# Hybrid encoder layer on one core: query and key/value latents computed together, block by block of the input features

## The chip, the cores and the metric

One core of one Trainium2 chip runs the whole layer. The metric is the device time of one execution in microseconds, the median of several timed runs. A profile comes from one execution of its own, recorded by the hardware profiler; its span is somewhat shorter than the timed figure, because the timed figure takes in what lies around the span.

## The reference

One layer of an encoder, for 512 tokens of 1024 features, everything float32:

```python
h = RMSNorm(x); z = h @ W_in     # columns: q-latent 256 | kv-latent 256 | rotary key 64 |
                                 #          HGRN2 q 512 | f_fwd 512 | f_bwd 512 | i 512 | gate 512
q = rms_norm(rms_norm(c_q, g_qa) @ w_qb, g_qn)       # 4 heads of 128 + 64 rotary
k, v from rms_norm(c_kv, g_kva) @ w_kvb              # 4 heads of 128 (+ shared rotary key), v 128
A = softmax(q k^T * 192**-0.5) v                     # dense, both directions in time
B = HGRN2: gated linear recurrence, chunks of 64, one scan forward and one backward, summed
x += concat(A, B) @ W_o
x += SwiGLU(RMSNorm(x))                              # inner width 2816
x += sigmoid(RMSNorm(x) @ W_pg) * (p[layer] @ W_pp)
```

The gates of HGRN2 are f = lower + (1 - lower) * sigmoid(z), where `lower` comes from a softmax over two rows of learned bounds.

## The kernel before

**Precision.** Every float32 factor is split into a high and a low part (`split`: ScalarE copies or scales to the high part, VectorE subtracts to get the low part). A product of two such factors is three products on TensorE (`mm3`, L137 to L139: hi·hi, hi·lo, lo·hi). A chunk of weights is loaded by the SyncE queue (SP) into one of four `raw` buffers and split into one of three pairs of buffers `whi`, `wlo` (`weights`).

**Order.** Each engine runs its instructions in one fixed order. This order is found before the launch by a scheduler that goes by the program's dependences and by its own picture of durations, so an edit in one place can move instructions elsewhere. An engine stands still while its next instruction waits, and all that is queued behind it stands too.

**Front part.** x lies transposed in eight blocks of 128 features by 512 tokens (`xT[k]`, 256 KB each). VectorE, ScalarE and GpSimd (POOL) set constants, and TensorE does `WARM` products of constants (`warm`). Then:

1. the query's latents `cq` in two banks, as features by tokens: per block k the parts `hh`, `hl` of x times gain (`vec` holds the gains), and 2 x 3 products of 512 columns. w_q comes in five loads, for blocks (0), (1), (2,3), (4,5), (6,7);
2. constants `cst`, `row`, `pos` are loaded, and POOL makes the sum of the squares of x (`sq`, `sqacc`);
3. the key/value latents `ckv` in four banks, as tokens by features: per block 4 x 3 products of 320 columns, with w_kv in three loads;
4. `token_rstd` turns the squares into 1/rms (`ss`), the latents are normed (`squares`, `cT`, `ctok`), POOL and ScalarE make the rotary tables, and the bounds of the gates (`lower`) are worked out from columns 30 to 45 of `vec`.

**Middle part** (some 40 to 300 us). Two streams share TensorE: the attention (`rk`, `ropeT`, `qkT` are transposes; `ks`, `kl`, `qs` are the rotary parts of key and query, `qkh`, `qkl` the other parts; `s` are scores, `p` their exponentials, `pT` these transposed, `av` the values) and the projections of HGRN2 (`wi`, one tile of 128 columns is 24 products against a weight chunk of 1024 columns). VectorE serves both: it subtracts the low parts of the weights (`wlo`, L131), evacuates tiles (`z`), runs the scans of the gates (L636, L638), copies their decays in small pieces (`dm`, `dt`), finishes `qs` (L484), and takes maxima of scores.

**Last part.** Output projection, feed-forward (`ff`, `dn`), per-layer gate (`pg`).

Of the kernel before, what the change touches and what calls it, by code (L numbers as in the profile page):

```python
# [18 lines left out]
KT = 8  # L19
# [5 lines left out]
# shares of the two streams  # L25
# [5 lines left out]
WARM = 7  # L31
# [5 lines left out]
# columns of the packed per-partition vectors  # L37
V_MIX, V_FFN, V_PLE, V_QA, V_KVA, V_QN, V_KN, V_LB, V_HGO = 0, 8, 16, 24, 26, 28, 29, 30, 46
NV = 50
# columns of the packed rows (the same for every partition)  # L40
R_QN, R_KN = 0, 64
NR = 128
# columns of the constants that depend on shapes alone
# [11 lines left out]
class Slots:  # L55
    """Tiles of one size, handed out by hand: the one that has been free longest comes next."""
# [19 lines left out]
    def part(self, prefix, n):  # L76
        """Slots of their own from the free ones."""
        s = Slots(self.pool, 0, self.prefix)
        s.free.extend(self.free.popleft() for _ in range(n))
        s.count = 1000 * ord(prefix)  # L80
        return s
# [7 lines left out]
def merge(streams):  # L89
    """Runs generators side by side, by the shares of their totals that they have yielded. One that  # L90
    yields a condition waits until it holds."""
# [16 lines left out]
def v3(t, a, b=None):  # L108
    """A tile's 512 columns as (a, b)."""
    return t.rearrange("p (a b) -> p a b", a=a)  # L110
# [3 lines left out]
def layer_kernel(ctx: ExitStack, tc: tile.TileContext, io, out):  # L114
# [11 lines left out]
    # ---------------------------------------------------------------- helpers  # L126
    def split(hi, lo, src, scale=None, eng=dve):
        """src (times a scale per partition) = hi + lo, each exact in float32r."""
# [14 lines left out]
    def weights(src, cols, lo_eng=None):  # L143
        """A chunk of weights [128, cols]: its parts hi and lo."""
# [14 lines left out]
    def rsqrt_mean(o, ss, n):  # L159
        """o = (ss / n + eps) ** -0.5, for a few columns."""  # L160
# [5 lines left out]
    def token_rstd(sq, keep=None):  # L166
        """From sums of squares [128 of the features, tokens]: 1/rms by token, tokens on
        partitions [128, 4] and on columns, the same on every partition [128, 512]."""
# [6 lines left out]
        # the diagonal matrices of 1 / rms, summed over the partitions  # L175
# [13 lines left out]
    def squares(acc, src, first):  # L189
        """acc += src ** 2"""  # L190
# [8 lines left out]
    # ---------------------------------------------------------------- inputs  # L199
# [3 lines left out]
    sp.dma_start(vec, io["vec"])  # L203
# [7 lines left out]
    # loads the activation engine's table while the first inputs are under way  # L211
    act.activation(small.tile([P, 1], F32, tag="first", name="first"), mhalf[:, :1], AF.Exp)

    # ---------------------------------------------------------------- input projection, latents
    # the query's latents, features on partitions
    hT = [(A.get(f"hh{k}", F32R), A.get(f"hl{k}", F32R)) for k in range(KT)]
    cq = [B.get(f"cq{m}") for m in range(2)]
    # the tensor engine's clock rises while it is busy
# [4 lines left out]
    for ks in ((0,), (1,), (2, 3), (4, 5), (6, 7)):  # L223
        w = weights(io["w_q"][:, ks[0] * 256 : (ks[-1] + 1) * 256], len(ks) * 256)
        for k in ks:
            if k:
                sp.dma_start(xT[k], io["xT"][k])
            split(hT[k][0], hT[k][1], xT[k], vec[:, V_MIX + k : V_MIX + k + 1])
            for m in range(2):
                o = (k - ks[0]) * 256 + m * P  # L230
                mm3(cq[m], cut(w, o, o + P), hT[k], k == 0, k == KT - 1)
# [10 lines left out]
    for k in range(KT):  # L242
        t = A.get("sq") if k else sq
        pool.tensor_tensor(t, xT[k], xT[k], ALU.mult)
        if k:
            pool.tensor_tensor(sq, sq, t, ALU.add)
            A.put(t)
    A.put(*xT)

    # those of key and value and the rotary key, tokens on partitions  # L250
    ckv = [B.get(f"ckv{j}") for j in range(NT)]
    for c, ks in enumerate(((0, 1, 2), (3, 4, 5), (6, 7))):
        w = weights(io["w_kv"][:, ks[0] * 320 : (ks[-1] + 1) * 320], len(ks) * 320)
        for k in ks:
            for j in range(NT):
                o = (k - ks[0]) * 320
                mm3(ckv[j][:, :320], cut(hT[k], j * P, (j + 1) * P), cut(w, o, o + 320), k == 0, k == KT - 1)
# [16 lines left out]
    # ---------------------------------------------------------------- rotary tables  # L274
# [17 lines left out]
    # cos(r) = sin(pi / 2 - |r|)  # L292
# [9 lines left out]
    def rope(eng, o, x, c, s, t1, t2):  # L302
        """o = x * [cos, cos] + [x2, x1] * [-sin, sin], all [128, a, 64]"""
# [5 lines left out]
    # ---------------------------------------------------------------- lower bounds of the gates  # L309
    lb = vec[:, V_LB : V_LB + 16]  # L310
# [13 lines left out]
    # ================================================================ latent attention  # L324
# [4 lines left out]
    def attention():  # L329
        """Emits the attention in pieces; yields the tensor engine's time for each."""  # L330
        # 1 / rms of the latents, with the one of the input
        sc = cpool.tile([P, 2 * NT], F32, name="sc")  # by token: query, key and value
# [28 lines left out]
        # the shared rotary key, with its gains, turned  # L361
# [8 lines left out]
        def wsmall(name, cols):  # L370
            """A small matrix of two chunks, two halves each."""
# [11 lines left out]
        # keys and values; per head, tokens on partitions: [128, tile, 128]  # L383
# [3 lines left out]
        rt = [A.get(f"rk{j}") for j in range(NT)]  # rotary parts by tile: [128, (key, query) x head, 64]  # L387
# [164 lines left out]
    q, kk, bb = {}, {}, {}  # L552
    gg, vv = [], []

    # chunks of weights for the dense stream, one ahead of its use
    wlist = deque()
    ahead = deque()
    nd = [0]
# [520 lines left out]
```

## Time and profile before

| what | us |
|---|---|
| timed runs | 723.92 median (723.46, 723.92, 724.87) |
| span of the profiled execution | 721.8 |
| TensorE busy | 703.6 (97%) |
| VectorE busy | 439.3 (61%) |
| ScalarE busy | 309.2 (43%) |
| GpSimd busy | 135.8 (19%) |

The profile gives the profiled execution's time as its span, 721.8 us; no other time of that execution is shown. The median of the timed runs lies 2.1 us above it. Busy shares are means over the span, so they say little about a stage. "Idle before, releaser" is the time an engine stood and what ended it. PEclk is TensorE's granted clock as a share of full speed.

### The profile page before, as it was taken

The page shows a single profiled execution, that of the slowest core. Times are in us where ns is not written, and L with a number is a line of the kernel's source. Part 1 is how long each engine was busy: PE and PEld are TensorE (multiplying, and loading weights), DVE is VectorE, ACT ScalarE, POOL GpSimd, SP SyncE. Part 2 cuts the span into 40 slices and gives each one's busy share as a digit, 9 for nine tenths or more (in the row PEclk, how much of TensorE's full clock was granted, in tenths as well). Part 3 has the DMA queues.
Part 4 walks back from the last instruction along what each step waited for, and adds up shares of the span by engine and source line. Part 5 has one row for each costly group of instructions (what it writes and reads, how often), then busy time and mean ns, then how long its engine had stood idle before and what let it go on. Part 6 is the DMA issues. An engine that isn't in the chain of part 4 may idle for free.

```text
span 721.8 us, 9167 instructions
## 1 busy us (share of the span) xinstructions
PE 703.6 (97%) x3516; PEld 588.5 (82%) x3516; DVE 439.3 (61%) x733; ACT 309.2 (43%) x573; POOL 135.8 (19%) x126
## 2 busy tenths in 40 slices
PE   8999997998999999999999999999999999999997
PEld 6888885897878888788888888888888888888886
DVE  8954469988999984386545334435433444456573
ACT  5566785576554635355233222223222223244341
POOL 7983577010543511001000000000000000000000
PEclk9999999999999999999999999999999999999999
DMA  8432112111034221033232322232233232233211
GB/s 282 167 114 93 59 36 81 59 30 60 15 103 156 60 78 59 30 118 116 96 109 87 104 101 87 91 114 77 79 108 117 90 108 87 78 105 116 89 59 58
DMA packets 22075, 66.36 MB, mean 92 GB/s; under 512 B 2704, under 2 KB 3984, under 8 KB 22032
## 3 DMA queue, kind: packets, MB, share of 16 engines
q1 hardware_dynamic: 22032, 65.79, 28.0%
q8 instruction: 27, 0.44, 0.2%
q14 instruction: 16, 0.13, 0.1%
HBM read 63.68 MB, written 2.10 MB: 91 GB/s over the span
## 4 chain that ended last, share of the span: by engine, by line
PE 85%; DVE 8%; ACT 3%; DMA 2%; issue 1%; SPq 1%; POOL 0%; ACTq 0%; POOLq 0%
PE ff L137 11%; PE ff L138 11%; PE ff L139 11%; PE dn L138 6%; PE dn L137 6%; PE dn L139 6%; PE wi L139 3%; PE wi L137 3%; PE wi L138 3%; PE pg L139 2%; PE pg L138 2%; PE pg L137 2%; PE wo L137 2%; PE wo L139 2%; PE wo L138 2%; PE po L787 1%
## 5 line engine op out<-in xcount | busy, mean ns | idle before, releaser
L130 ACT ACTIVATE whi<-raw 128x1024 fp32r<-128x1024 f32 (+4 forms) x114 | 116.2, 1019 | 286.6 <-issue 103.1
L131 DVE TENSOR_TENSOR wlo<-raw,whi 128x1024 fp32r<-128x1024 f32 (+4 forms) x108 | 133.7, 1240 | 26.1 <-ACT whi L130 24.8
L137 PE MATMUL ff<-hh,whi 128*128 128x512 f32 x352 | 137.0, 390 | 0.1
L138 PE MATMUL ff<-hl,whi 128*128 128x512 f32 x352 | 136.8, 389 | 0.0
L139 PE MATMUL ff<-hh,wlo 128*128 128x512 f32 x352 | 136.8, 389 | 0.0
L957 DVE TENSOR_TENSOR z<-ff,rsbc 128x512 f32<-128x512 f32 x44 | 30.1, 691 | 109.8 <-PE ff L139 109.2
L164 POOL TENSOR_TENSOR rs_tok<-rs_v,mhalf 128x4 f32<-128x4 f32 x3 | 4.7, 1568 | 391.7 <-DVE rs_v L163 391.7
L137 PEld LDWEIGHTS ff<-hh,whi 128*128 128x128 f32 x352 | 66.1, 188 | 14.3 <-ACT whi L130 0.5
L138 PEld LDWEIGHTS ff<-hl,whi 128*128 128x128 f32 x352 | 66.1, 188 | 13.7
L139 PEld LDWEIGHTS ff<-hh,wlo 128*128 128x128 f32 x352 | 66.1, 188 | 13.6
L137 PE MATMUL dn<-ah,whi 128*128 128x512 f32 x176 | 68.5, 389 | 0.0
L138 PE MATMUL dn<-al,whi 128*128 128x512 f32 x176 | 68.5, 389 | 0.0
L139 PE MATMUL dn<-ah,wlo 128*128 128x512 f32 x176 | 68.5, 389 | 0.0
L139 PE MATMUL wi<-hh,wlo 128*128 128x512 f32 x128 | 51.7, 404 | 3.6 <-DVE wlo L131 3.6
L926 DVE TENSOR_TENSOR x<-x,dn 128x512 f32<-128x512 f32 x24 | 16.5, 687 | 60.5 <-PE dn L139 60.5
L138 PE MATMUL wi<-hl,whi 128*128 128x512 f32 x128 | 51.4, 401 | 0.0
L137 PE MATMUL wi<-hh,whi 128*128 128x512 f32 x128 | 51.0, 400 | 0.0
L137 PEld LDWEIGHTS dn<-ah,whi 128*128 128x128 f32 x176 | 33.0, 188 | 6.9
L139 PEld LDWEIGHTS dn<-ah,wlo 128*128 128x128 f32 x176 | 33.0, 188 | 6.8
L138 PEld LDWEIGHTS dn<-al,whi 128*128 128x128 f32 x176 | 33.0, 188 | 6.8
L139 PEld LDWEIGHTS wi<-hh,wlo 128*128 128x128 f32 x128 | 24.5, 191 | 8.9 <-DVE wlo L131 4.0
L138 PEld LDWEIGHTS wi<-hl,whi 128*128 128x128 f32 x128 | 24.4, 191 | 4.9
(287 smaller groups left out, 1361.9 us busy)
## 6 DMA issues: line engine op xcount, KB each, us to landing
raw<-in_w_gate SPq DMA_DIRECT2D x22, 512.0 KB, 3.3
raw<-in_w_up SPq DMA_DIRECT2D x22, 512.0 KB, 3.2
raw<-in_w_hf SPq DMA_DIRECT2D x16, 512.0 KB, 3.7
raw<-in_w_d SPq DMA_DIRECT2D x16, 448.0 KB, 3.2
x<-in_xT SPq DMA_DIRECT2D x16, 256.0 KB, 5.2
raw<-in_w_d SPq DMA_DIRECT2D x8, 512.0 KB, 3.3
raw<-in_w_pg SPq DMA_DIRECT2D x8, 512.0 KB, 3.2
raw<-in_w_i SPq DMA_DIRECT2D x4, 512.0 KB, 3.4
```

Of the source, the lines that this page charges most:

```text
L130: act.activation(hi, src, AF.Copy)
L131: eng.tensor_tensor(lo, src, hi, ALU.subtract)
L137: pe.matmul(o, lhsT=l[0], rhs=r[0], start=start, stop=False)
L138: pe.matmul(o, lhsT=l[0], rhs=r[1], start=False, stop=False)
L139: pe.matmul(o, lhsT=l[1], rhs=r[0], start=False, stop=stop)
L164: pool.tensor_tensor(o, v[:, :w], mhalf[:, :w], ALU.pow)
L787: pe.matmul(po[:, ts(j)], lhsT=l, rhs=r, start=n == 0, stop=n == len(terms) - 1)
L926: dve.tensor_tensor(xT[m], xT[m], o, ALU.add)
L957: dve.tensor_tensor(z, o, bc2, ALU.mult)
```

## The change

For each block k the kernel now loads x, the block's 256 columns of w_q and the block's 320 columns of w_kv into one `raw` buffer, splits these 576 columns together (block 0 in two parts), and does the query products and the key/value products of that block; the key/value products of the last two blocks come after both queries. `vec` is loaded behind the first w_q block. The squares of x are made by `squares`, which is the function that the latents used already: ScalarE squares, VectorE adds. The bounds of the gates come from a load of their own, `vlb`, behind `cst`, `row` and `pos`. `WARM` is 10 in place of 7. The rest of the diff takes comments out.

```diff
-WARM = 7
+WARM = 10
...
     vec = cpool.tile([P, NV], F32, name="vec")
-    sp.dma_start(vec, io["vec"])
...
-    for ks in ((0,), (1,), (2, 3), (4, 5), (6, 7)):
-        w = weights(io["w_q"][:, ks[0] * 256 : (ks[-1] + 1) * 256], len(ks) * 256)
-        for k in ks:
-            if k:
-                sp.dma_start(xT[k], io["xT"][k])
-            split(hT[k][0], hT[k][1], xT[k], vec[:, V_MIX + k : V_MIX + k + 1])
-            for m in range(2):
-                o = (k - ks[0]) * 256 + m * P
-                mm3(cq[m], cut(w, o, o + P), hT[k], k == 0, k == KT - 1)
+    ckv = [B.get(f"ckv{j}") for j in range(NT)]
+    ws = []
+
+    def load_k(k):
+
+        if k:
+            sp.dma_start(xT[k], io["xT"][k])
+        raw = wpool.tile([P, 1024], F32, tag="raw", bufs=RAWB, name=f"rawl{k}")
+        hi = wpool.tile([P, 1024], F32R, tag="whi", name=f"whil{k}")
+        lo = wpool.tile([P, 1024], F32R, tag="wlo", name=f"wlol{k}")
+        sp.dma_start(raw[:, :256], io["w_q"][:, k * 256 : k * 256 + 256])
+        if k == 0:
+            sp.dma_start(vec, io["vec"])
+        sp.dma_start(raw[:, 256:576], io["w_kv"][:, k * 320 : k * 320 + 320])
+        for c in (slice(0, 256), slice(256, 576)) if k == 0 else (slice(0, 576),):
+            split(hi[:, c], lo[:, c], raw[:, c])
+            if c.start == 0:
+                split(hT[k][0], hT[k][1], xT[k], vec[:, V_MIX + k : V_MIX + k + 1])
+        ws.append((hi, lo))
+
+    def query_k(k):
+        for m in range(2):
+            mm3(cq[m], cut(ws[k], m * P, m * P + P), hT[k], k == 0, k == KT - 1)
+
+    def key_k(k):
+        for j in range(NT):
+            mm3(ckv[j][:, :320], cut(hT[k], j * P, j * P + P), cut(ws[k], 256, 576), k == 0, k == KT - 1)
+
+    for k in range(KT):
+        load_k(k)
+        query_k(k)
+        if k < KT - 2:
+            key_k(k)
+    for k in range(KT - 2, KT):
+        key_k(k)
...
     sq = A.get("sqacc")
     for k in range(KT):
-        t = A.get("sq") if k else sq
-        pool.tensor_tensor(t, xT[k], xT[k], ALU.mult)
-        if k:
-            pool.tensor_tensor(sq, sq, t, ALU.add)
-            A.put(t)
+        squares(sq, xT[k], k == 0)
     A.put(*xT)
-
-    ckv = [B.get(f"ckv{j}") for j in range(NT)]
-    for c, ks in enumerate(((0, 1, 2), (3, 4, 5), (6, 7))):
-        w = weights(io["w_kv"][:, ks[0] * 320 : (ks[-1] + 1) * 320], len(ks) * 320)
-        for k in ks:
-            for j in range(NT):
-                o = (k - ks[0]) * 320
-                mm3(ckv[j][:, :320], cut(hT[k], j * P, (j + 1) * P), cut(w, o, o + 320), k == 0, k == KT - 1)
+    vlb = cpool.tile([P, 16], F32, name="vlb")
+    sp.dma_start(vlb, io["vec"][:, V_LB : V_LB + 16])
...
-    lb = vec[:, V_LB : V_LB + 16]
+    lb = vlb
```

**Place A: the start of TensorE.** Names are bank or tile and version: `cq_1` and `cq_2` are the banks of the query's latents, `hh_9` and `hl_10` the parts of block 0, `whi_116` or `whil_122` the high parts of its weights. Before:

```order
L221 MATMUL warm_107<-ones 128x128 x7
L137 MATMUL cq_1_105<-hh_9_89,whi_116 128x512
L137 MATMUL cq_2_106<-hh_9_89,whi_116 128x512
L138 MATMUL cq_1_105<-hl_10_90,whi_116 128x512
L138 MATMUL cq_2_106<-hl_10_90,whi_116 128x512
L139 MATMUL cq_1_105<-hh_9_89,wlo_117 128x512
```

And now, on the same engine at the same place:

```order
L220 MATMUL warm_106<-ones 128x128 x10
L137 MATMUL cq_1_104<-hh_9_88,whil_122 128x512
L137 MATMUL cq_2_105<-hh_9_88,whil_122 128x512
L137 MATMUL ckv_4_117<-whil_122,hh_9_88 128x320
L137 MATMUL ckv_5_118<-whil_122,hh_9_88 128x320
L137 MATMUL ckv_6_119<-whil_122,hh_9_88 128x320
L137 MATMUL ckv_7_120<-whil_122,hh_9_88 128x320
L138 MATMUL cq_1_104<-hl_10_89,whil_122 128x512
```

The key/value products of block 0 now stand between the query's products of the high parts and those of the low parts, and ten warming products stand ahead.

**Place B: VectorE during the gates.** `k`, `t` and `z` belong to the gates of the four heads and directions, `rk` to the rotary parts; `wlo_1469` before and `wlo_1484` now is the low part of the same chunk of weights, which the next tile `wi` (`wi_1581`, now `wi_1596`) waits for. Line numbers of the changed kernel are 15 higher here. Before:

```order
L618 TENSOR_SCALAR k_1199<-z_646 128x512
L627 TENSOR_SCALAR t_1212<-z_646 128x512
L445 TENSOR_TENSOR rk_88_573<-pq_76019_1033,rq 128x128
L576 TENSOR_TENSOR z_1395<-wi_1318,rsbc_385 128x512
L628 TENSOR_SCALAR z_812<-z_812 128x512
L480 TENSOR_TENSOR kl_1099<-ropeT_1093,ks_1098 64x512
L628 TENSOR_SCALAR z_722<-z_722 128x512
L628 TENSOR_SCALAR z_646<-z_646 128x512
L131 TENSOR_TENSOR wlo_1469<-raw_1467,whi_1468 128x1024
```

And now:

```order
L591 TENSOR_TENSOR z_1410<-wi_1333,rsbc_400 128x512
L131 TENSOR_TENSOR wlo_1484<-raw_1482,whi_1483 128x1024
L633 TENSOR_SCALAR k_1214<-z_661 128x512
L642 TENSOR_SCALAR t_1227<-z_661 128x512
L643 TENSOR_SCALAR z_827<-z_827 128x512
L460 TENSOR_TENSOR rk_88_588<-pq_76018_1047,rq 128x128
L460 TENSOR_TENSOR rk_88_588<-pq_76019_1048,rq 128x128
L643 TENSOR_SCALAR z_737<-z_737 128x512
```

The low part of the weights now stands ahead of a `k`, a `t`, the two last `rk` and the three `z` of the gates, behind which it stood.

**Place C: the first scores.** `s_1253` before and `s_1268` now is the first head's first block of scores; its products with `qs` need the rotary part of the query, which comes from `ropeT_1110` (now `ropeT_1125`) by way of VectorE. Before, the last transpose into `ropeT_1110` stood 24 rows ahead of the first product with `qs_1115` on TensorE. Now, on TensorE:

```order
L139 MATMUL wi_1488<-hh_23_102,wlo_1414 128x512
L487 MATMUL ropeT_1125<-cst,rk_88_588 128x128
L137 MATMUL s_1340<-qkh_1180,qkh_1171 128x512
L138 MATMUL s_1340<-qkl_1181,qkh_1171 128x512
L139 MATMUL s_1340<-qkh_1180,qkl_1172 128x512
L524 MATMUL s_1268<-ks_1113,qs_1130 128x512
```

Three products lie between them now. On VectorE, `qs` stood before among the copies of the decays:

```order
L636 SCALAR_TENSOR_TENSOR t_1212<-mF_447,z_646 128x512
L684 COPY dm<-t_1212 128x8
L685 TENSOR_TENSOR dm<-t_1212 128x8
L686 COPY dm<-t_1212 128x8
L684 COPY dm<-t_1215 128x8
L484 TENSOR_TENSOR qs_1115<-ropeT_1110,qs_1115 64x512
```

And now it stands at their end, behind 32 of them and a chunk of weights (`wlo_1796`):

```order
L720 COPY dt<-dm 128x4
L721 TENSOR_TENSOR dt<-dm 128x4
L722 TENSOR_TENSOR dt<-dm 128x4
L131 TENSOR_TENSOR wlo_1796<-raw_1794,whi_1795 128x1024
L499 TENSOR_TENSOR qs_1130<-ropeT_1125,qs_1130 64x512
```

Between `wlo_1469` and `qs_1115` VectorE had four scans, three `qkl`, two `kl`, one evacuation and four small copies. Between `wlo_1484` and `qs_1130` it has the same four scans, two `kl` and one evacuation, one `qkl` more, the eight gate and `rk` instructions that place B shows to have moved, `wlo_1664` as well as `wlo_1796`, and 28 small copies more. TensorE has 58 products of 512 columns and 13 transposes between its first product with `wlo_1484` and its first with `qs_1130`.

## Rows read from the trace of the kernel before

**Rows 1.** The page: busy us and share of each engine, number of instructions.

```profile
PE 703.6 (97%) x3516; PEld 588.5 (82%) x3516; DVE 439.3 (61%) x733; ACT 309.2 (43%) x573; POOL 135.8 (19%) x126
PE 85%; DVE 8%; ACT 3%; DMA 2%; issue 1%; SPq 1%; POOL 0%; ACTq 0%; POOLq 0%
```

**Rows 2.** Stage by stage: stretch, its length, busy us (instructions), granted clock, DMA share, GB/s.

```profile
core 0: us, PE busy (x) PEld busy (x) DVE busy (x) ACT busy (x) POOL busy (x), PEclk, DMA share, GB/s
...
5.32:10.16 4.84, 4.84 (x12) 3.80 (x13) 4.76 (x10) 3.09 (x6) 4.00 (x3) 1.00 0.96 285
10.16:22.45 12.29, 9.47 (x39) 6.55 (x38) 12.29 (x9) 6.25 (x10) 12.29 (x10) 1.00 0.88 317
22.45:36.52 14.07, 14.07 (x97) 14.07 (x96) 12.84 (x12) 8.42 (x15) 13.72 (x14) 1.00 0.46 148
...
112.49:119.33 6.84, 3.28 (x8) 2.61 (x9) 6.78 (x8) 4.48 (x8) 6.84 (x6) 0.75 0.24 77
...
166.97:174.00 7.03, 4.25 (x19) 3.50 (x19) 7.03 (x19) 4.06 (x9) 0.00 (x0) 0.76 0.30 89
```

**Rows 3.** The same view, three microseconds after the first long wait.

```profile
116.00:119.00 3.00, 2.95 (x7) 2.38 (x8) 2.97 (x4) 1.02 (x2) 3.00 (x3) 0.50 0.55 175
```

**Rows 4.** TensorE's waits, 0 to 60 us: total us, times, longest.

```profile
PE cq L138 <- DVE hl L134: 2.7, 2, 1.5
PE cq L137 <- ACT whi L130: 0.9, 1, 0.9
```

**Rows 5.** TensorE's waits, 60 us to the end.

```profile
PE wi L139 <- DVE wlo L131: 3.6, 1, 3.6
PE pT L529 <- ACT p L515: 2.8, 1, 2.8
PE av L138 <- DVE pTl L131: 1.3, 1, 1.3
```

**Rows 6.** TensorE in order of time: start, us, line, operation, idle before.

```profile
1.04 3.35 PE L221 MATMUL warm<-ones 128*128 128x128 f32 x14 [1.04 <-DVE ones L206]
5.32 1.22 PE L137 MATMUL cq<-hh,whi 128*128 128x512 f32 x2 [0.93 <-ACT whi L130]
```

**Rows 7.** ScalarE in order of time.

```profile
3.61 0.72 ACT L133 ACTIVATE hh<-x,vec 128x512 fp32r<-128x512 f32 x1 [1.39 <-DMA vec<-in_vec]
4.85 0.42 ACT L130 ACTIVATE whi<-raw 128x256 fp32r<-128x256 f32 x1 [0.53 <-DMA raw<-in_w_q]
```

**Rows 8.** VectorE in order of time, at the start.

```profile
4.68 0.74 DVE L134 SCALAR_TENSOR_TENSOR hl<-x,vec,hh 128x512 fp32r<-128x512 f32 x1
```

**Rows 9.** VectorE's instructions by form, 0 to 40 us: busy us, mean ns.

```profile
L134 DVE SCALAR_TENSOR_TENSOR hl<-x,vec,hh 128x512 fp32r<-128x512 f32 x8 | 9.7, 1244 | 0.0
L196 DVE TENSOR_TENSOR sqc<-sqc,sq 128x512 f32<-128x512 f32 x1 | 0.8, 772 | 0.0
```

**Rows 10.** GpSimd's instructions by form, 0 to 40 us.

```profile
L246 POOL TENSOR_TENSOR sqacc<-sqacc,sq 128x512 f32<-128x512 f32 x7 | 11.0, 1575 | 0.1
```

**Rows 11.** Loads issued from 0 to 40 us: KB each, median us to landing.

```profile
raw<-in_w_q SPq DMA_DIRECT2D x2, 128.0 KB, 3.2
```

**Rows 12.** VectorE's instructions by form, 100 to 150 us.

```profile
L131 DVE TENSOR_TENSOR wlo<-raw,whi 128x1024 fp32r<-128x1024 f32 x4 | 5.9, 1485 | 0.0
...
L638 DVE TENSOR_TENSOR_SCAN t<-mF,z 128x512 f32<-128x512 f32 x2 | 3.7, 1833 | 0.0
...
L636 DVE TENSOR_TENSOR_SCAN t<-mF,z 128x512 f32<-128x512 f32 x2 | 2.7, 1374 | 0.0
```

**Rows 13.** VectorE in order of time, from the awaited low part to `qs`.

```profile
113.70 2.29 DVE L131 TENSOR_TENSOR wlo<-raw,whi 128x1024 fp32r<-128x1024 f32 x1
...
126.45 0.16 DVE L685 TENSOR_TENSOR dm<-t 128x8 f32<-128x8 f32 x1
126.53 0.16 DVE L686 COPY dm<-t 128x8 f32<-128x8 f32 x1
...
126.80 0.69 DVE L484 TENSOR_TENSOR qs<-ropeT,qs 64x512 fp32r<-64x512 f32 x1
```

## The prediction

> **What bounds the kernel now.** I read the page's engine shares first: TensorE is busy 97% of the span and makes 85% of the chain that ended last [rows 1]. The products themselves don't change, so all that an edit can move is what TensorE loses: time in which it stands, and time in which it runs slowly. That is why I went next to the table by stage [rows 2] and to the waits [rows 4, 5].
>
> The stage table shows where the loss of the front part lies. From 22.45 to 36.52 us 97 instructions fill 14.07 us without a gap: 0.145 us for a product of 320 columns, hence about 0.232 us for one of 512. The 48 query products and 96 key/value products need 48 x 0.232 + 96 x 0.145 = 25.1 us at that pace. The stretch from the first of them (5.32 us [rows 6]) to the end of the last (36.52) is 31.2 us, so 6.1 us are lost. Of these, 2.1 lie in 5.32 to 10.16, where 12 products take 4.84 us in place of 2.8: about half pace, although the granted-clock column says 1.00 there; I go by the products. 2.7 are two waits of TensorE for `hl`, a low part that VectorE makes [rows 4]; they fall into 10.16 to 22.45, where VectorE and GpSimd are both busy all the time (12.29 of 12.29 each) and TensorE is busy 9.47. The other 1.3 are small. Outside this, 5.3 us stand ahead of the first product, 0.93 of them after warming had ended [rows 6].
>
> The middle part loses as much in three waits [rows 5]: 3.6 us for `wlo`, 2.8 for `p`, 1.3 for `pTl`. After each of the two long ones TensorE comes back at half its clock, 1.2 of 2.4 GHz: granted 0.50 from 116 to 119 us [rows 3]. Over the two stretches the mean is 0.75 of 6.84 us and 0.76 of 7.03 us [rows 2], so each fall costs about a quarter of 7 us, 1.7 us. Together 11.1 us.
>
> **The change part by part.**
>
> *Warming products and first data.* 14 instructions of seven products take 3.35 us, 0.24 each [rows 6]; ten products are 20 instructions, 4.8 us, ending at 5.83 rather than 4.39. Before, TensorE then stood 0.93 us for the high weights; now the data must be compared: `hh` can start at 3.6 as before or somewhat later, since `vec` is loaded after w_q; a w_q block of 128 KB takes 3.2 us to land [rows 11] and is issued one load earlier; ScalarE now has one square (0.72 at most, as `hh` [rows 7]), `whi` (0.42) and `hh` (0.72) ahead of the first product. From 3.4 to 3.6 these end between 5.3 and 5.9. So the start is at 5.9, +0.6 us. If nothing of the slow pace is saved, these 0.6 are a plain loss.
>
> *The slow pace.* TensorE sped up in the front part at 10.16 us, 4.84 us after a gap of 0.93; after the two long waits of the middle part half pace lasted 3 to 3.5 us of work. With no gap between warming and products, I take it that the pace rises near the end of warming, leaving 0.4 of the 2.1 us. Bounds: 0 left, or all of 2.1 if it rises at 10.2 again whatever went before.
>
> *Blocks together.* TensorE now has 6 x 0.232 + 12 x 0.145 = 3.13 us of work per block. What has to be supplied in that time: ScalarE `hh` 0.72, a square at most 0.72, `whi` of 576 columns at most 0.42 x 576/256 = 0.94: 2.4 us. VectorE `hl` 0.74 when GpSimd is quiet [rows 8], the add 0.77 [rows 9], `wlo` about 0.75: 2.3 us. Loads 256 + 128 + 160 KB, 557,000 bytes: at the 285 to 317 GB/s of the front [rows 2] 1.8 to 2.0 us. All are below 3.13, and three pairs of weight buffers and eight of `hh`, `hl` let them run ahead, so no wait is due once the first block is in. Then the two waits of 2.7 us go, and most of the small ones.
>
> *Squares from GpSimd to ScalarE and VectorE.* GpSimd loses seven adds of 1.575 us [rows 10] and eight squares. While they ran, `hl` took 1.24 us in the mean against 0.74 alone [rows 8, 9]. So VectorE gains more by the quiet than the seven adds cost (5.4 us). GpSimd's rotary work stays, from about 15 us on, and can stretch VectorE's 2.3 us per block to 2.3 x 1.24/0.74 = 3.9, more than 3.13, for the last few blocks; being ahead should hide it. I put 0.3 us, between 0 and 4 x 0.8 = 3.2.
>
> *24 block loads in place of 16, a load for `vlb`.* They hang on the load stream alone, which needs some 2.0 us per block against TensorE's 3.13: nothing. The bounds `lower` are needed only by the gates near 100 us, so their later load costs nothing either; if it came late VectorE would stand in its queue with the last low parts behind it, a few us at most.
>
> The Trainium skill, "DMA: Bandwidth & Descriptors", section "Bandwidth", speaks against the smaller loads: it gives a transfer as about 2.0 us fixed plus its bytes at 436 GB/s, so that 128 KB run far below the peak. By that page, were each load to wait for the last, a block would be estimated at 2.6 + 2.3 + 2.4 = 7.3 us, and the latents would end near 64 us. This trace disagrees for a queue of loads: 285 to 317 GB/s were moved while loads of 128 and 256 KB were in flight [rows 2], so several overlap.
>
> *Sum of the front.* Start 5.9, products 25.1, slow rest 0.4, VectorE 0.3, small gaps 0.3: the latents end at 32.0 in place of 36.5, a gain of 4.5 us (2.3 to 5.9 by the bounds of clock and small waits).
>
> **Middle part.** The order moves there too, though no line of it was edited. Place B: `wlo` stands ahead of `k`, `t` (0.34 apart each in VectorE's stream), three `z` and two `rk`, some 2.6 us; TensorE waited 3.6 for it. It comes about 1.0 us late now, and the fall of the clock behind it may go: -2.6 - 1.7 = -4.3. Place C: VectorE needed 11.5 us before from the end of `wlo` (113.70 + 2.29 = 115.99) to the end of `qs` (126.80 + 0.69 = 127.49) [rows 13]; to this the new order adds one `qkl` 0.7, the 2.6 us that moved, two chunks at 1.49 [rows 12] and 28 small copies 0.08 apart [rows 13], 2.2: 20.0 us, of which four scans are 6.4 [rows 12]. TensorE has 58 x 0.232 + 13 x 0.12 = 15.0 us of work meanwhile (a transpose has 128 columns as the warming instructions have, 0.24 us at half pace [rows 6]). It will stand up to 5.0 us for `qs`, and not at all if VectorE is ahead by that much; I take 4.8, near the upper end, since VectorE is busy 6.78 of 6.84 us just there [rows 2], plus 1.7 for the clock: +6.5. What is late next: the scores, the softmax, the values. The second stall (2.8 + 1.3 + 1.7 = 5.8) should shrink to about 2, as TensorE's wait at `qs` lets VectorE and ScalarE catch up, but 1.8 of it may return at the first values, which have no `wi` products between them now: -2.0. The middle comes to +0.2 us, with 4 us either way.
>
> **Sum.** 721.8 - 4.5 + 0.2 = 717.5 us of span; the timed median lay 2.1 above the span, so 719.6.
>
> **Rivals.** What a measurement here can tell from no change is about 0.2%, 1.45 us.
>
> 1. *Forecast*: front gains 4.5, the middle nets out within 2 us: 717.5 to 721.6. Chance 0.47.
> 2. *Middle better*: TensorE doesn't stand at `qs`, since VectorE, relieved of place B and of GpSimd's disturbance, is there in time. Then the -4.3 and the -2.0 add to the front's gain: 721.8 - 4.5 - 6.3 + 2.1 = 713.1, or up to 717.5 with a part of the wait left. For it: place B frees 2.6 us ahead. Against it: VectorE hardly rests there. Chance 0.21.
> 3. *Front eaten*: the wait at `qs` keeps its 6.5 and the second stall stays whole: +2.2 to +5; 721.6 to 725.4, no change. Against it: VectorE and ScalarE work on while TensorE stands at `qs`. Chance 0.15.
> 4. *Slower*: `qs` costs 6.5, and the softmax behind it makes a further long wait with its own fall of the clock (2.8 + 1.7), while the second stall stays: 721.8 - 4.5 + 2.2 + 4.5 + 3 + 2.1 = 729. It decides once the middle loses more than 6 us net, as the front's gain is then gone. Chance 0.09.
> 5. *Change doesn't do what it says*: the pace rises only at 10.2 (+1.7) and VectorE starves the last blocks (+3): the front gains nothing, 723 to 724. Chance 0.07.
> 6. *Loads starve TensorE*: were they to come one after another, at 3.2 us for each of the three of a block [rows 11], loading takes 8 x 9.6 = 77 us, the latents end at 80 and the kernel takes some 768. The rate in [rows 2] excludes it nearly. Chance 0.01. This is the case that the Trainium skill's page on DMA speaks for.
>
> Faster means below 722.5: cases 1, 2 and the low end of case 3 (0.04), 0.72. The same: the rest of case 3 and case 5, 0.18. Slower: 0.10. From 714.6 to 724.6 leaves out a third of case 2 (0.07), the upper end of case 3 (0.03), and cases 4 and 6: 2 in 10.
>
> **What would show it.** The profile after should show the first query product at 5.9, products 0.23 apart by 7 us, no wait for `hl`, `ss` at 32, and SyncE's loads done before 20. In the middle: no wait of 3.6 for `wlo`, a wait of 4 to 5 us of `s` for `qs` with a granted clock of 0.5 behind it, and a second stall below 3. The prediction is wrong if TensorE waits for `hl` or loads after block 1, or if the waits of the middle come to much more or less than the 11.1 us of before.

## The result, and the profile after

The changed kernel takes 732.42 us (median of 4 runs, 731.43 to 734.41) against 724.19 (723.46 to 724.87): 1.012 times the time before, interval 1.0108 to 1.0132. It is slower by 8.2 us, where 719.6 was forecast. The profiled span is 732.6 against 721.8; the profiled execution was the slowest of the four (734.41), so the two profiles differ by 10.8 us and not by 8.2.

The page's shares, busy time and then the chain that ended last, answer to [rows 1]:

```profile
PE 709.5 (97%) x3522; PEld 593.2 (81%) x3522; DVE 431.6 (59%) x741; ACT 313.1 (43%) x582; POOL 113.6 (16%) x111
PE 81%; DVE 9%; issue 5%; ACT 3%; POOL 2%; POOLq 0%; DVEq 0%; ACTq 0%
```

TensorE's own part of the chain fell from 85% to 81%: more of it is now set by others. Of the 10.8 us that the span grew, TensorE stands 4.9; the other 5.9 are busy time (709.5 against 703.6 us) for the same products and six more warming instructions, so more than half of the loss is a slower pace and not waiting. TensorE's waits from 0 to 60 us, and then from 60 us to the end (total us, times, longest), answer to [rows 4, 5]:

```profile
PE ct L371 <- ACT c L285: 4.1, 2, 3.8
...
PE av L138 <- DVE pTl L131: 3.9, 2, 2.3
PE s L524 <- DVE qs L499: 3.5, 1, 3.5
PE wi L137 <- DVE z L591: 2.0, 1, 2.0
PE s L137 <- DVE qkl L134: 1.6, 1, 1.6
PE pT L544 <- ACT p L530: 0.7, 1, 0.7
PE s L138 <- DVE qkl L134: 0.4, 1, 0.4
```

The waits for `hl` and for `wlo` are gone, as forecast. There is one new wait that no part of the forecast named, 4.1 us of `ct` for `c`, and the middle has a chain of four waits for `qkl`, `z` and `qs` where one was expected. The stages:

```profile
core 0: us, PE busy (x) PEld busy (x) DVE busy (x) ACT busy (x) POOL busy (x), PEclk, DMA share, GB/s
10.00:30.80 20.80, 20.80 (x122) 19.16 (x121) 16.42 (x30) 13.88 (x25) 10.38 (x16) 1.00 0.86 282
30.80:36.48 5.68, 1.55 (x13) 1.18 (x11) 1.88 (x3) 5.43 (x12) 1.52 (x2) 0.86 0.19 72
36.48:42.00 5.52, 5.52 (x15) 4.33 (x16) 4.58 (x12) 3.13 (x10) 3.09 (x2) 0.53 0.43 142
...
100.00:140.00 40.00, 32.26 (x134) 24.13 (x133) 33.07 (x72) 24.27 (x43) 21.50 (x19) 0.88 0.19 66
```

Row by row: the front runs without a gap, 20.80 of 20.80 us. Then TensorE does 1.55 us of work in 5.68, and comes back at a granted 0.53, that is mostly at 1.2 of its two levels of 1.2 and 2.4 GHz: 5.52 x (1 - 0.53) = 2.6 us lost. From 100 to 140 us TensorE is busy 32.26 of 40 and VectorE 33.07; in the kernel before they are busy 35.37 and 38.61 there.

TensorE in order of time (start, us, line, operation, idle before) shows the front's success and its end:

```profile
5.25 0.73 PE L137 MATMUL cq<-hh,whil 128*128 128x512 f32 x2 [0.25 <-ACT hh L133]
...
6.73 0.39 PE L138 MATMUL cq<-hl,whil 128*128 128x512 f32 x1
6.96 0.40 PE L139 MATMUL cq<-hh,wlol 128*128 128x512 f32 x1
...
30.80 0.94 PE L171 MATMUL ss<-ones,sqacc 128*128 128x1 f32 x8
35.53 0.48 PE L371 MATMUL ct<-cst,c 128*128 128x128 f32 x1 [3.79 <-ACT c L285]
36.48 0.77 PE L137 MATMUL wi<-hh,whi 128*128 128x512 f32 x1
```

The latents end at 30.80 us, 5.7 earlier than the 36.52 of before [rows 2]. But the first product behind the handover, `wi`, starts at 36.48; in the kernel before it starts at 37.50. So 4.7 of the 5.7 us are gone before the middle begins. The slow clock behind it takes the rest: the lag of the same `wi` and score products against before is +1.1 to +1.4 us for most of 43 to 56 us, +1.3 at 104, +9.5 at the first product with `qs` (137.15 against 127.63), about +9 from 180 to 217 us, and +10.6 to +10.7 from 219 us to the end. Two places lose most of the time: the handover and the stretch from 104 to 137. The last 1.6 us are a fall of the clock behind a wait of 1.5 us for `pTl` (granted 0.66 from 225 to 230 us of this profile).

### The profile page after: what moved, and what is told of

It reads as the page before. It is cut to its first block, busy times and chain, and to the rows that moved or that the text cites. A ratio compares the mean times of both kernels' runs of the same rounds, so it can differ in the third digit from the quotient of the medians.

```text
span 732.6 us, 9206 instructions
## 1 busy us (share of the span) xinstructions
PE 709.5 (97%) x3522; PEld 593.2 (81%) x3522; DVE 431.6 (59%) x741; ACT 313.1 (43%) x582; POOL 113.6 (16%) x111
## 4 chain that ended last, share of the span: by engine, by line
PE 81%; DVE 9%; issue 5%; ACT 3%; POOL 2%; POOLq 0%; DVEq 0%; ACTq 0%
PE ff L138 11%; PE ff L137 11%; PE ff L139 11%; PE dn L138 5%; PE dn L137 5%; PE dn L139 5%; PE wi L137 3%; PE wi L138 3%; PE wi L139 3%; PE pg L139 2%; PE pg L137 2%; PE pg L138 2%; PE wo L137 2%; PE wo L138 1%; PE wo L139 1%
## 5 line engine op out<-in xcount | busy, mean ns | idle before, releaser
L130 ACT ACTIVATE whi<-raw 128x1024 fp32r<-128x1024 f32 (+1 forms) x106 | 110.9, 1047 | 269.0 <-issue 96.5
L131 DVE TENSOR_TENSOR wlo<-raw,whi 128x1024 fp32r<-128x1024 f32 (+1 forms) x100 | 120.2, 1203 | 28.9 <-ACT whi L130 27.8
L139 PE MATMUL ff<-hh,wlo 128*128 128x512 f32 x352 | 136.8, 389 | 0.0
L139 PEld LDWEIGHTS ff<-hh,wlo 128*128 128x128 f32 x352 | 66.1, 188 | 13.7
L139 PE MATMUL dn<-ah,wlo 128*128 128x512 f32 x176 | 68.5, 389 | 0.0
L137 PE MATMUL wi<-hh,whi 128*128 128x512 f32 x128 | 53.2, 416 | 2.0 <-DVE z L591 2.0
L139 PE MATMUL wi<-hh,wlo 128*128 128x512 f32 x128 | 52.5, 410 | 0.0
L139 PEld LDWEIGHTS dn<-ah,wlo 128*128 128x128 f32 x176 | 33.0, 188 | 6.9
L137 PEld LDWEIGHTS wi<-hh,whi 128*128 128x128 f32 x128 | 25.4, 199 | 7.6 <-DVE z L591 2.6
L139 PEld LDWEIGHTS wi<-hh,wlo 128*128 128x128 f32 x128 | 25.3, 198 | 5.9 <-DVE wlo L131 0.7
```

What stands on the lines that cost most here:

```text
L130: act.activation(hi, src, AF.Copy)
L131: eng.tensor_tensor(lo, src, hi, ALU.subtract)
L137: pe.matmul(o, lhsT=l[0], rhs=r[0], start=start, stop=False)
L139: pe.matmul(o, lhsT=l[1], rhs=r[0], start=False, stop=stop)
```

## The experiments

**Theory.** (a) The front gains about 5 us. (b) At the handover ScalarE, whose instructions run in a fixed order, has the rotary tables and splits of later weights ahead of the copies `c` of the key/value latents; `ct` stands ahead of all `wi` on TensorE, so TensorE waits, and its clock falls. (c) The changed order of the middle costs the rest. **Rivals**: the slow part is in the new front itself; or the waits named by the trace only move when one is taken away.

For (b), here is ScalarE at the handover of the changed kernel. The latents end at 30.80, and the first copy `c` starts 4.3 us later:

```profile
30.23 1.28 ACT L311 ACT_TABLE_LOAD   x1
...
34.12 1.05 ACT L130 ACTIVATE whi<-raw 128x1024 fp32r<-128x1024 f32 x1
35.06 0.42 ACT L285 COPY c<-ckv 128x320 f32<-128x320 f32 x1
```

To tell front from order, the instructions of each engine behind the latents were chained in a given order, by edges that order without adding a wait between engines. The kernels below differ in the table `ROWS` and in the lines named:

```diff
+def pin(tc, n):
+    traced = [i for i in tc.nc.cur_bb.bb.instructions if "PoolBoundary" not in type(i).__name__][-n:]
+    info = lambda: mybir.DependencyInfo(mybir.DependencyClass.NoSync, mybir.DependencyReason.DATA)
+    for text in ROWS.values():
+        last = None
...
+                if last is not None:
+                    tc.add_manual_dep(traced[j], traced[last].name, info(), reason="order")
+                last = j
...
+        pin(tc, 4607)
```

### Front and order apart

**The new front with the order of before** (the changed kernel, `ROWS` from the kernel before):

> The changed front part, with each engine's instructions behind it (from the sums of squares on) held in the order of the kernel before. Theory (the front gained 5.7 us, and what lies behind it lost 16 because its order changed): 724.2 - 5.7 = 718.5 us, between 717 and 720, with no wait of the transposes ct for ScalarE's copies above 0.5 us. Rival (the change itself slows what follows, by its load stream or by the work that VectorE and ScalarE took over, whatever the order): at least 728.

725.58 us, ratio 1.0013 (1.0002 to 1.0025): no gain to speak of, so the theory's 718.5 failed, and the rival's 728 did not come either. The latents end at 31.14, as (a) says. TensorE's longest wait of the first 60 us and ScalarE in order of time:

```profile
PE ct L371 <- ACT c L285: 3.1, 1, 3.1
...
27.60 1.27 ACT L133 ACTIVATE cTh<-cq,vec 128x512 fp32r<-128x512 f32 x2 [4.92 <-PE cq L139]
34.75 1.39 ACT L285 COPY c<-ckv 128x320 f32<-128x320 f32 x4
```

The order of before was right for latents that end at 36.5, when the copies were just in time. With latents 5.4 us earlier, `c` still starts at 34.75, behind splits that stood ahead of it. From 36 to 40 us the granted clock is 0.50. The first `wi` starts at 35.67, still 1.8 us ahead of before; by 44 us the slow clock has made that 0.5 us behind. The handover alone eats the front's gain.

**The old front with the order of the changed kernel** (the kernel before, `ROWS` from the changed one):

> The front part of before, with everything behind it in the order of the changed kernel. Theory (the order is what costs): 724.2 plus 8.2 for the change of the median plus the 5.7 that the front had gained, about 738, between 733 and 741. Rival (the change itself): 724, within 1.5.

741.48 us, ratio 1.0247 (1.0231 to 1.0263), just above the range. The order costs 17.7 us on the old front (741.48 - 723.78), 0.8 of them ahead of the end of the latents (37.35 against 36.52); the longest wait of `ct` is 7.5 there.

**Seven warming products** (the first of these with `WARM = 7`):

> As the first run of this call, with seven warming products in place of ten. Theory (a gap ahead of the first product keeps TensorE at half pace until about 10 us): 1.5 to 2.5 us slower than that run. Rival (the pace rises at the same time either way): within 0.5 us of it.

724.29 us, 1.0003 (0.999 to 1.0017). The latents end 1.1 us later (`ss` at 32.26), yet the kernel isn't slower, which neither forecast had. The handover does not absorb the delay: the wait for `c` is 3.1 us in both, and the first `wi` starts 1.06 us later too (36.73 against 35.67). The clock makes up for it: from the first `wi` to 45 us the mean granted clock is 0.84 here and 0.72 with ten, and by 42 us the two run level. So the worth of the warming products can't be read from these two times.

### The handover

**The rotary tables behind the copies** (the changed kernel's order, on ScalarE alone):

```diff
-ACTIVATE tmp<-ang / ACT_TABLE_LOAD / ACTIVATE sn<-ang x2 / ACTIVATE cc<-tmp
 ACTIVATE cTh x2 ... COPY c<-ckv x4
+ACTIVATE tmp<-ang / ACT_TABLE_LOAD / ACTIVATE sn<-ang x2 / ACTIVATE cc<-tmp
```

> The changed kernel in its own order on every engine, but ScalarE's four steps for the rotary tables (with their table load) stand behind its copies of the key/value latents, not ahead. Theory (the handover from the latents to the first tile costs 4.1 us of waiting and some 2.4 of half clock, and they stay lost): 732.4 - 6 = 726.5, between 725.5 and 727.5. Rival (VectorE sets the end of the middle part, so what is saved here is waited for later): 730 to 732.4.

727.63 us, 1.0057 (1.0042 to 1.0073): 4.8 us better than the changed kernel, just above the range. Two smaller waits remain, in the same view:

```profile
PE bc L181 <- DVE dgh L178: 1.4, 1, 1.4
PE ct L371 <- ACT c L285: 1.2, 2, 0.7
```

**The whole handover mended, order of before.** On ScalarE the five splits that TensorE needs first stand ahead of `cTh`, and `c` right behind the squares of the query's latents; VectorE and GpSimd follow suit:

```diff
+ACT wsh x4, whi_525
 ACT cTh x2
-ACT wsh x2
 ACT sqc, sq
-ACT wsh x2, whi_525, wsh_855, whi_531
 ACT c x4
+ACT wsh_855, whi_531
...
+DVE wsl x4, wlo_526 (ahead of cTl), rs_v (ahead of wsl_856); POOL rs_tok (ahead of wlo_532)
```

> The first run's kernel (changed front part, order of before behind it), with ScalarE and VectorE doing the weights of the next stage while they wait for the query's latents, and the four copies of the key/value latents right behind the latents' squares; GpSimd's 1/rms ahead of its share of weights. Theory (the handover ate the front's gain, 3.1 us of waiting for the copies and some 2.4 of half clock): 725.6 - 5.3 = 720.3, between 719 and 721.5, faster than the kernel before. Rival (the gain of the front is waited for once more at a later place of the middle part, where VectorE sets the pace): 724 to 725.6.

718.03 us, ratio 0.992 (0.9907 to 0.9933): faster than both kernels by 6.4 and 14.4 us, and better than expected. TensorE in order of time:

```profile
31.33 0.95 PE L171 MATMUL ss<-ones,sqacc 128*128 128x1 f32 x8
32.14 0.42 PE L371 MATMUL ct<-cst,c 128*128 128x128 f32 x2
32.31 0.48 PE L137 MATMUL wi<-hh,whi 128*128 128x512 f32 x1
```

No wait, no fall of the clock, and `wi` 5.2 us before that of the kernel before. This is what the front was worth there; the lead is still 5.1 us at 166. The rest of the 6.4 comes behind the wait for `p`, where the kernel before has a granted 0.76 [rows 2] and this profile 1.00.

**The same mend with the changed kernel's order of the middle.** Two runs of one kernel; the second gave the profile, since the profiled execution of the first took 2925 us and is left out of its comparison:

> The changed kernel with its own order of the middle part, and the handover mended on ScalarE, VectorE and GpSimd as in the fifth run. So it differs from the fifth run by the order of the middle part alone. Theory (the order of the middle part costs by itself, whatever comes before): 725.6, between 724.5 and 727, so 7 to 9 us above the fifth run's 718.0. Rival (the rest of the loss lies in the handover and not in the middle): 718 to 721.

726.52 us, 1.0026 (1.0011 to 1.0041).

> The ninth run's kernel once more, since its profiled execution took 2925 us and shows nothing. By the theory (the order of the middle part costs by itself) the first tile starts within 0.5 us of the fifth run's 32.3 us, the lag behind that run is below 1 us until 100 us, and grows by 7 to 9 us between 100 and 240 us, half of it standing and half of it at half clock. By the rival (the handover) the lag is there at 50 us.

724.67 us in its one run, the span 722.9 against 716.0 for the mended kernel above. Its `wi` starts at 31.61 against 32.31, so its handover is as good, and at 94 us it is 0.2 behind. At the first product with `qs` it is 8.1 behind (130.76 against 122.65), and 7.0 to 7.8 from 134 to 213 us. The order of the middle alone costs 726.52 - 718.03 = 8.5 us (runs of 723.7 to 728.4 against 717.6 to 718.4); in these two profiles it is 6.9 us of span, all of it lost between 94 and 131 us.

Timed, the change thus splits into -6.4 for front and mended handover (718.03 against its own 724.44 of before), +8.5 for the order of the middle, and 732.42 - 726.52 = +5.9 for the unmended handover. That these add up to +8.0 is no check, since each difference starts where the last one ended. Taken in another order the shares are others: with the order of before, the unmended handover costs 725.58 - 718.03 = 7.6 and the order on top of it 732.42 - 725.58 = 6.8.

### Inside the middle

**One wait taken away in the order of before.** In the mended kernel `wlo` of place B moves ahead of three `z` and a `kl` on VectorE, which is part of what the changed order does there:

```diff
 DVE z_1410<-wi_1333
+DVE wlo_1484<-raw_1482,whi_1483
 DVE z_827 / kl_1114 / z_737 / z_661
-DVE wlo_1484<-raw_1482,whi_1483
```

> The fifth run's kernel with one instruction moved: VectorE makes the low part of the weights that TensorE waits 3.55 us for ahead of one kl and three z of the gates, 2.4 us earlier. Theory of the prediction (a wait taken away at this place stays away): 718.0 - 2.4 = 715.6, between 715 and 716.6. Rival (VectorE and TensorE wait for each other in turn, and what moved behind the weights is waited for next): 717 to 719.

718.37 us, 0.9917 (0.9902 to 0.9931): nothing. TensorE's waits, 30 to 300 us, and the stage windows of this kernel; the last row is the same window of the kernel without the move:

```profile
...
PE wi L137 <- DVE z L591: 1.6, 1, 1.6
PE qkT L474 <- DVE rk L460: 0.9, 1, 0.9
PE qkT L474 <- DVE kl L495: 0.9, 1, 0.9
PE s L524 <- DVE qs L499: 0.8, 1, 0.8
PE s L138 <- DVE qkl L134: 0.5, 1, 0.5
PE wi L139 <- DVE wlo L131: 0.2, 1, 0.2
...
100.00:140.00 40.00, 34.91 (x159) 26.53 (x158) 38.78 (x98) 23.58 (x45) 15.28 (x11) 1.00 0.20 66
```

```profile
100.00:140.00 40.00, 35.44 (x160) 28.11 (x159) 38.77 (x98) 23.63 (x45) 15.37 (x11) 0.96 0.21 66
```

The 3.5 us for `wlo` are gone, and 3.8 come back at `z`, `qkl`, `kl` and `qs`, all of them VectorE's. The column to look at is VectorE's: 38.78 and 38.77 of 40 us, the same 98 instructions. The clock no longer falls there either (1.00 against 0.96), and that gains nothing too. In this stretch VectorE sets the pace, and which of its products TensorE waits for makes no difference.

**The changed order, seen the same way.** Here are VectorE's waits from 100 to 148 us in the kernel with mended handover and changed order, and two windows:

```profile
DVE z L591 <- PE s L139: 2.8, 1, 2.8
...
100.00:140.00 40.00, 32.22 (x127) 23.97 (x126) 34.83 (x79) 19.48 (x36) 15.11 (x12) 0.87 0.19 59
...
127.00:135.00 8.00, 4.55 (x13) 3.38 (x12) 3.72 (x17) 2.22 (x4) 0.00 (x0) 0.57 0.21 68
```

Now VectorE stands too: 34.83 of 40. From 127 to 135 us TensorE first waits 3.5 us for `qs`, then runs 13 products, with a mean granted clock of 0.57 over the stretch, while VectorE stands 2.8 us. The releaser named is a product of the scores (`s`, L139), which ends just before `z` starts; no `wi` runs in between, so it is the scores that `z` waits for (why, the profile doesn't say). In the mended kernel with the order of before, VectorE's longest wait from 100 to 148 us is 0.6. Here each waits for the other in turn, and neither works on in the meantime. That is how an order loses time that no single wait shows.

**`qkl` and `qs` earlier** (the kernel with the tables moved; `ropeT` ahead of the first scores on TensorE, and on VectorE and ScalarE):

```diff
 DVE qkl_1172
+DVE qkl_1181
 DVE wlo_1664 / t_1227
+DVE qs_1130 / qs_1133
...
-DVE qkl_1181 (behind 10 dm copies)
-DVE qs_1130 / qs_1133 (behind wlo_1796)
```

> The changed kernel with the rotary tables behind the copies, as in the third run, and at the first scores one transpose of ropeT, the two casts and two subtractions of qs, and one qkl moved ahead of the copies of the decays and two chunks of weights. Theory (TensorE's waits there, 1.6 us for qkl and 3.5 for qs, and the half clock behind them, some 2 us, are a loss of the order): 727.6 - 6 = 721.6, between 720 and 724. Rival (VectorE has more work than TensorE there, so TensorE waits for the next thing): 726 to 728.

725.65 us, runs of 721.9 to 728.6, 1.0011 (0.9991 to 1.0031): between the two forecasts. The profiled execution (727.37) shows the rival's case:

```profile
PE wi L137 <- DVE z L591: 5.4, 2, 3.4
...
PE s L524 <- DVE qs L499: 0.6, 1, 0.6
```

The wait for `qs` fell from 3.4 to 0.6 us and that for `qkl` vanished; a second wait for `z`, 3.4 us, took their place. What VectorE did not do while it made `qs` early it owes as `z`. From 94 to 170 us VectorE is busy 63.0 of 76 us here and 61.9 without the move, but 70.0 in the mended kernel with the order of before: it stands nearly as long as it did. Four of the twelve runs, at a mean clock of 0.997, took only 721.9 to 723.6, inside the theory's range; none of them was profiled, so whether the move gains something when the clock holds stays open.

### Inside the front

**The squares back on GpSimd**, in the mended kernel:

```diff
-        squares(sq, xT[k], k == 0)
+        t = A.get("sq") if k else sq
+        pool.tensor_tensor(t, xT[k], xT[k], ALU.mult)
+        if k:
+            pool.tensor_tensor(sq, sq, t, ALU.add)
+            A.put(t)
```

> As the first run of this call, with the squares of x on GpSimd as they were before; the rest of the front as changed. Theory (the waits for hl went because query and key/value products of a block stand together, 3.1 us of TensorE work to a block): the latents end within 0.5 us, but GpSimd is done with its sums later, so the wait for ss or for the tables grows: 0 to 3 us slower. Rival (they went because GpSimd no longer slows VectorE): TensorE waits for hl again, 2 us or more, and the latents end that much later.

724.44 us, 1.0008 (0.9997 to 1.0019): all of the gain is gone. My theory, that the grouping by blocks gave VectorE the slack, fell; the rival held, though TensorE now waits for the low part of the weights and not for `hl`. The longest wait, 0 to 60 us, and VectorE's forms up to 38 us (busy us, mean ns), with the squares on GpSimd:

```profile
PE cq L139 <- DVE wlol L131: 4.0, 6, 1.2
...
L134 DVE SCALAR_TENSOR_TENSOR hl<-x,vec,hh 128x512 fp32r<-128x512 f32 x8 | 11.2, 1424 | 1.3 <-ACT hh L133 1.3
L131 DVE TENSOR_TENSOR wlol<-rawl,whil 128x576 fp32r<-128x576 f32 x7 | 10.1, 1450 | 0.0
```

And the same two forms with the squares on ScalarE:

```profile
L134 DVE SCALAR_TENSOR_TENSOR hl<-x,vec,hh 128x512 fp32r<-128x512 f32 x8 | 6.0, 749 | 1.3 <-ACT hh L133 1.3
L131 DVE TENSOR_TENSOR wlol<-rawl,whil 128x576 fp32r<-128x576 f32 x7 | 5.4, 765 | 0.0
```

The same instructions take 1424 and 1450 ns beside GpSimd's squares, 749 and 765 without: 15 instructions lose 10 us of VectorE, and the latents end 6.1 us later (37.42 against 31.33). The Trainium skill, "GPSIMD Engine Reference", section "Specifications", says that GpSimd's access to SBUF is shared with VectorE and contends with VectorE instructions that have two SBUF inputs; both forms have two, and these rows agree with it.

**The squares alone**, in the kernel before (`squares(sq, xT[k], k == 0)` in place of the GpSimd lines, seven warming products, the queries first):

> The kernel before with one part of the change, the squares of x by ScalarE with adds on VectorE; all else as it was, order left to the scheduler (some ten instructions stand elsewhere). Theory (the waits for hl came from GpSimd slowing VectorE): the two waits of 2.7 us go, hl takes about 0.75 us, and the time is 724.2 - 2.7 = 721.5, between 720.5 and 722.5. Rival (without the blocks together the loads bind, and the handover takes back what is gained): 723.5 to 725.

722.25 us, 0.9975 (0.9956 to 0.9995), in two clusters, 719.4 to 720.9 and 723.6 to 725.6, so the median stands for neither, and neither forecast is settled by it. What the profile (723.62) shows is clear: the waits for `hl` are gone, `hl` takes 746 ns and the latents end at 33.19, 3.3 us earlier. Again the handover takes most of it: a wait of `ct` for `c` of 2.5 us with a mean clock of 0.72 behind it, 36 to 42 us.

**Seven warming products** in the mended kernel (`WARM = 7`):

> As the first run of this call, with seven warming products. Theory (half pace lasts longer): the latents end 1.1 us later, as in the fourth run, and with no long wait behind them the time is 0.8 to 1.5 us longer. Rival (it is absorbed in the waits of the middle part): within 0.4 us.

720.34 us, 0.9948 (0.9936 to 0.996): 2.3 slower than with ten, more than expected. TensorE in order of time:

```profile
4.92 1.22 PE L137 MATMUL cq<-hh,whil 128*128 128x512 f32 x2 [0.52 <-ACT hh L133]
...
7.00 0.63 PE L138 MATMUL cq<-hl,whil 128*128 128x512 f32 x1
7.43 0.63 PE L139 MATMUL cq<-hh,wlol 128*128 128x512 f32 x1
```

With ten:

```profile
5.87 0.96 PE L137 MATMUL cq<-hh,whil 128*128 128x512 f32 x2 [0.20 <-ACT hh L133]
...
7.26 0.39 PE L138 MATMUL cq<-hl,whil 128*128 128x512 f32 x1
7.49 0.39 PE L139 MATMUL cq<-hh,wlol 128*128 128x512 f32 x1
```

Behind a gap of 0.52 us the products are 0.43 us apart until 8.7 us; with ten and a gap of 0.20 they start 0.95 later but are 0.23 apart from 7.26. The first `wi` starts 1.4 us later; small waits make that 1.8 by 106 us, and the rest, to 2.5 at the end, is a fall of the clock at 166 us that the other profile doesn't have (below).

## Why the prediction was wrong

- **Front, forecast -4.5 us.** The waits went as forecast, and that was worth more: the latents end 5.7 us earlier in the changed kernel, and 5.2 arrive at the first `wi` when the handover is mended. Of the steps, the start came at 5.25 rather than 5.9 (5.2 to 6.2 over the profiles with ten warming products), the slow pace ended near the end of the warming products, as taken, and no wait for `hl` or `wlol` is left. The step "blocks together" gave it the wrong cause: the slack comes from the squares' leaving GpSimd, which the part on squares saw (1.24 against 0.74 us) but priced as a remark. Counted from the first product to the end of the latents, the kernel before takes 31.2 us; blocks together with the squares on GpSimd 31.2 (6.20 to 37.42); the squares alone moved 27.1 (6.06 to 33.19); both 26.6 with seven warming products (5.71 to 32.26) and 25.8 with ten (5.33 to 31.14). Most of it is the squares, so that the size came near was in part luck.
- **Loads.** Right. The front moved 282 GB/s, and the loads' medians (issue to landing) were these:

```profile
rawl<-in_w_q SPq DMA_DIRECT2D x8, 128.0 KB, 4.1
x<-in_xT SPq DMA_DIRECT2D x8, 256.0 KB, 4.4
```

  A load of twice the bytes takes 0.3 us more, with several in flight. The Trainium skill's page "DMA: Bandwidth & Descriptors" (section "Anatomy of one DMA — SWDGE (gpsimd) path", not "Bandwidth", as the prediction has it) gives 2.0 us fixed plus bytes at 436 GB/s, fitted to loads that GpSimd issues; these are SyncE's. By that figure an estimate for one alone is 2.3 and 2.6 us: the step of 0.3 agrees, the rest is longer here, and loads one after another, the rival of the forecast, didn't come.
- **Handover, forecast 0.** This step was not in the sum at all. "The latents end at 32.0 in place of 36.5, a gain of 4.5 us" took the end of one stage for the start of the next. What stood ready at 36.5 us in the kernel before had to be ready at 31, and ScalarE's queue was not looked at there. Cost: 5.9 us timed; the profile shows 4.1 us of waits and 2.6 of slow clock.
- **Middle, place B, forecast -4.3.** The wait did go, and the gain with it did not stay: moved by itself it gave 0 (718.37 against 718.03). The forecast read VectorE's 6.78 busy of 6.84 us [rows 2] and used it for place C, but not here, where it says that VectorE sets the pace and a wait for it can only move.
- **Middle, place C, forecast +6.5.** The wait for `qs` was put at 4.8 us plus 1.7 of clock. Measured were 3.5, but also 2.0 for `z` and 2.0 for `qkl`, and a mean clock of 0.88 from 100 to 140 us, where the kernel before has 0.96. The wait that was forecast came, and smaller; the two beside it were not in the sum. What was missing is that VectorE stands as well (33.07 busy us against 38.61 before), so that its time is lost.
- **Second stall, forecast -2.0.** The wait for `p` fell to 0.7 us and that for `pTl` rose to 3.9: 4.6 in place of 4.1 [rows 5]. It moved, and the clock fell behind the last of these waits, where it held in the kernel before.
- In sum, the middle was put at +0.2 "with 4 us either way" and is +8.5. The rival "slower" had the right sign and came nearest in size (729 against 732.4), with 0.09, but by a further wait in the softmax that did not come about. Rival 3 came nearest in its mechanism (the wait at `qs` stays, the second stall too) and ended too low since it lacked the handover. Two slips in the sums changed nothing: that rival's upper end is 724.4 by its own terms, not 725.4, and the start worked out from 3.4 to 3.6 us ends at 5.3 to 5.5, not 5.9.

What stays open: which of the moved instructions in the middle starts the waiting in turn. Moving `wlo` alone in the order of before only moved the wait, and so did `qs` and `qkl` in the profiled execution; a full mend of the changed order was not tried. That VectorE's standing is what costs the time there is read from the profiles and was not taken away by itself.

## What to carry to other kernels

When a stage ends earlier, look at what the next stage's first instruction needs and what stands ahead of it in each engine's fixed order: a gain is worth only as much as that queue can follow. Before a wait is priced as a gain, look at the busy share of the engine waited for over the whole stretch; where it is near full (38.8 of 40 us here), taking a wait away moves it, and an order that lets that engine stand can make things worse. Where a scheduler orders the program, measure an edit with the old order kept as well: here one edit held -6.4, +8.5 and +5.9 us at once.

## What the runs showed of the hardware

**A wait of the same length sometimes costs the clock and sometimes not.** TensorE's wait for `p` is 2.78 us in the mended kernel and in the same with seven warming products. The 8 us from shortly before its end in the one, then in the other:

```profile
164.00:172.00 8.00, 6.66 (x45) 5.66 (x46) 8.00 (x19) 6.39 (x13) 0.00 (x0) 1.00 0.41 134
```

```profile
166.00:174.00 8.00, 7.48 (x41) 6.46 (x41) 8.00 (x19) 5.62 (x12) 0.00 (x0) 0.79 0.39 134
```

The granted clock stays 1.00 in the first and falls to a mean of 0.79 in the second. Likewise a wait of 1.5 us for `pTl` is followed by a mean of 0.66 from 225 to 230 us in the changed kernel, and by 1.00 throughout from 214 to 235 us in the one with the mended handover and the same order. It fits this that the runs of one kernel spread with their own mean clock: the new front with the order of before ran in 725.5 to 726.4 us at 0.985 (7 runs) and in 722.9 to 724.3 at 0.989 to 0.993 (5 runs). What decides it was not tested. A forecast that adds 1.7 us for each fall, as mine did, has that uncertainty in it, and a difference of 2 us between kernels with such waits needs many runs.

**After a long wait the pace doesn't fall at once.** Behind the 3.55 us for `wlo` in the mended kernel products start 0.23 us apart from 111.35 to 112.04, 0.43 apart from 112.32 to 115.31, and 0.23 again from 115.69.

**One execution of 2925 us.** In it `ff` products took 1099 ns in the mean against 389, all along the span, while the granted-clock figure for the core said 1.00. Nothing else here did this, and no cause is claimed.
